# Log decays and norm factors kept sixteen times in DRAM: spread loads that read sixteen places instead of one

## The chip, the core and the metric

The kernel runs on one core of a Trainium2 chip. The core has a matmul engine (PE, with weight loads shown apart as PEld), a vector engine (DVE), an activation engine (ACT), a general engine (POOL) and a sequencer that only issues transfers (SP). Transfers between DRAM and the on-chip memory run on sixteen DMA engines; most are issued by SP, some by POOL, a few by ACT. The on-chip memory has 128 partitions, and a matmul leaves its result in one of eight accumulation banks (here four named acc and four named dn). The metric is device time in microseconds, lower is better; a measurement is the median of several executions, and one execution more is taken with the profiler.

## The reference, cut to what matters

One decoder layer over 1024 positions of 2048 channels, in float32. The parts that the change touches are the first norm and the gated delta rule:

```python
h = rmsnorm(x, ln_g[l])                 # x * rsqrt(mean(x*x) + eps) * g, g has 2048 entries
proj = h @ w_in[l]                      # split into the groups' columns
...
g = -jnp.exp(dn_a_log[l]) * jax.nn.softplus(d_a + dn_dt_bias[l])    # log decays, 8 heads
...
g_cum = jnp.cumsum(g, axis=-1)
diff = g_cum[..., :, None] - g_cum[..., None, :]
decay = jnp.exp(jnp.where(tri, diff, -jnp.inf))
a = jnp.where(strict, jnp.einsum('bhnid,bhnjd->bhnij', kb, k) * decay, 0.0)
...
attn_intra = jnp.where(tri, jnp.einsum('bhnid,bhnjd->bhnij', q, k) * decay, 0.0)
q_g = q * jnp.exp(g_cum)[..., None]
```

Beside the delta rule there is a gated token mix (group A), attention into 256 memory tokens (group C), an output projection with a residual and a final norm. In all of these the matrix products carry nearly all of the work.

## The kernel before

Every float32 product is made of three products of rounded halves: an operand is split into a high part (a cast on ACT: whi, ahi, zh) and a low part (a subtraction on DVE: wlo, alo, zl), and PE adds hi*hi, hi*lo and lo*hi in a bank. Sequence positions go in two halves of 512; the large projections are made as seven products of sums of blocks instead of eight products.

The stages, in order of time: the keys and values of the memory (16 steps of k over w_mem_kv, 512 KB of weights each, in the rotating buffers wraw and ut); beside them the first norm of the x tiles (squares on ACT, a product of x with the row's factor and with gb, the spread ln_g, on DVE, a transpose on PE into the banks dn, a copy on ACT into tn, a split into ahi and alo); then the projections of the first four heads of the delta rule, the decays, and the per-head work; then the large projections with the scan of the delta rule between their products; at the end the output projection and the final norm.

The program text records operations; a planner (`Plan.issue`) sorts them by ready time, rank, and an estimated cost for each, and writes every engine's queue in that order. Engines execute their queues in order, so the planner's sequence decides who waits behind whom. `rank` sets a class (small goes first), `behind` holds an operation until another one in the planner's reckoning, without a wait on the chip. The estimates of a transfer depend on its size, on its longest run of bytes and on its issuer. All operations share one line in the profile, L297, the line of the planner that issues them, so rows are told apart by the names of their tiles.

The change touches two places:

- ln_g. Four loads on SP (`gb[c]`, the tiles zg) bring 512 entries each to all 128 partitions with `partition_broadcast(P)`: each of 128 partitions reads the same 2 KB of DRAM. They are recorded after step k = 3 of the memory's keys, with rank 2, and `prep` uses them for every x tile.
- the log decays. `decays(hf, a)` works out the cumulative log decays of a half for all heads, transposes them to rows (`gr`, 32 partitions of 128) and stores them on SP in `gcs[hf]` (gcd in the profile, 8 heads by 512 positions). For each head and half `qk` then issues on POOL a load of one row of 512 to all 128 partitions (`er`, the tile E): sixteen loads in all. ACT makes vs, the exponential of E, POOL masks E, and ACT makes the decay between positions from it.

Around the first place the queue of SP holds, in this order: x tile 0 (vs), weights of k = 7 (ut), weights of k = 8 (wraw, which waits until DVE has used up the buffer's former content), the four loads of ln_g (zg), weights of k = 9 (wraw), the four loads of x tile 1 (kd), weights of k = 10 and 11 (ut).

Of the kernel before, what the change touches and what calls it, by code (L numbers as in the profile page):

```python
# [17 lines left out]
P = 128  # L18
D = 2048
# [3 lines left out]
HT = 512  # L23
# [3 lines left out]
NG, NH, NX = 4, 8, 4  # L27
# [33 lines left out]
class Plan:  # L61
# [27 lines left out]
    @contextmanager  # L89
    def rank(self, cls):  # L90
        old, self.cls = self.cls, cls
        yield
        self.cls = old

    @contextmanager
    def behind(self, op):
        old, self.gate = self.gate, op
        yield
        self.gate = old
# [201 lines left out]
def kernel(  # L301
# [29 lines left out]
    V, S, G, PE, Q = R.dve, R.act, R.pool, R.pe, R.sp  # L331
# [5 lines left out]
    def DT(shape, name, dt=F32):  # L337
        return dr.tile(list(shape), dt, name=name, tag=name)[:]
# [38 lines left out]
    def rep(ap, n):  # L377
        return ap.unsqueeze(1).to_broadcast([ap.shape[0], n, ap.shape[1]])
# [42 lines left out]
    def tpb():  # L421
        turn["tp"] += 1
        return acc[2 + turn["tp"] % 2]

    h0_d = DT([KT, P, HT], "h0d")
    hT_d = DT([KT, P, HT], "hTd")

# [62 lines left out]
    gb = [ring["zg"]() for _ in range(4)]  # L490
# [4 lines left out]
    def load_mem(q):  # L495
        for mt in range(2):
            Q.dma_start(mem_rows[mt][q], mem[mt * P : (mt + 1) * P, q * HT : (q + 1) * HT])

    def kv_parts(k):
        n = XW if k == 0 else 2 * XW  # L500
        return [slice(i, i + n) for i in range(0, 2 * XW, n)]

    def load_kv(k):
        for sl in kv_parts(k):
            Q.dma_start(kvraw[k % 4][:, sl], w_mem_kv[k * P : (k + 1) * P, sl])
# [7 lines left out]
    y1 = C([P, 2 * NT, 32], "y1")  # L513
    rows = y1.rearrange("p c m -> p (c m)")[:, 0:P]
    mrow = rows[0:16]
    with rank(2):
        load_mem(0)
        S.dma_start(mrow, mem_norm_g[0].rearrange("(c p) -> c p", p=P))
        for k in range(4):
            load_kv(k)  # L520
            if k == 1:
                load_mem(1)
    with rank(3):
        load_mem(2)
        load_mem(3)
# [69 lines left out]
    for k in range(KT):  # L595
        mh, ml = mhl[k // 4]
        if k >= 4:
            with rank(3):
                load_kv(k)
        hi, lo = kvhi[k % 2], kvlo[k % 2]  # L600
        with rank(2):
            for sl in kv_parts(k):
                raw = kvraw[k % 4][:, sl]
                S.activation(hi[:, sl], raw, AF.Copy, scale=gcol[:, k : k + 1])
                V.scalar_tensor_tensor(lo[:, sl], raw, gcol[:, k : k + 1], hi[:, sl], op0=ALU.mult, op1=ALU.subtract)
        kk = k % 4
        for h in range(NX):
            sl = slice(h * P, (h + 1) * P)
            triple(ka[h][:, :NMEM], (hi[:, sl], lo[:, sl]), (mh[:, kk], ml[:, kk]), k == 0, k == KT - 1)
        for mt in range(2):  # L610
            sl = slice(mt * P, (mt + 1) * P)
            triple(va[mt], (mh[:, kk, sl], ml[:, kk, sl]), (hi[:, XW:], lo[:, XW:]), k == 0, k == KT - 1)
        kvmark.append(R.ops[-1])
        if k == 3:
            with rank(2), behind(kvmark[-1]):
                for c in range(4):
                    Q.dma_start(gb[c], ln_g[0, c * HT : (c + 1) * HT].partition_broadcast(P))
        if k in (1, 4, 8):
            with behind(kvmark[-1]):
                mhl.append(spread_mem(len(mhl)))  # L620
        if k == 1:
            load_x(0, "vs", kvmark[1:2] * 4)
        if k == 3:
            for mt in range(2):
                rm.append(C([P, 1], f"rm{mt}"))
                V.tensor_copy(rm[mt], row_scale(mem_rows[mt]))
        if k == 4:
            load_x(1, "kd", kvmark[4:5] * 4)
        if k == 5:
            prep(0, put0(0), spare)  # L630
        if k == 7:

            dg, rmb = (ring["E"]()[:, 0:NMEM] for _ in range(2))
            for mt in range(2):
                V.tensor_scalar(dg[:, mt * P : (mt + 1) * P], ident, rm[mt], None, op0=ALU.mult)
            pt = spare()
            PE.matmul(pt[:, 0:NMEM], ones, dg, start=True, stop=True)
            S.copy(rmb, pt[:, 0:NMEM])
        if k == 9:
            prep(1, put0(1), spare)  # L640
            load_x(2, "kT", (kvmark[6], kvmark[7], kvmark[7], kvmark[8]))
        if k == 13:
            load_x(3, "qT", (kvmark[10], kvmark[11], kvmark[11], kvmark[12]))
            with rank(2):
                prep(2, put0(2), spare)
# [6 lines left out]
    for mt in range(2):  # L652
        t = [ring["ai"](F32R) for _ in range(2)]
# [9 lines left out]
    for h in range(NX):  # L663
        t = ring["vs"](F32R).rearrange("p (s m) -> p s m", s=2)
# [105 lines left out]
    gr = C([NT * NH, P], "gr")  # L770
# [3 lines left out]
    r3, ww = ([steps[:, i * P : (i + 1) * P] for i in two] for two in ((0, 1), (2, 3)))  # L774
    scs = [C([P, 7, NT, NH], f"sc{hf}") for hf in range(2)]
    sct = C([P, 5, NT, NH], "sct")
    gcs = [DT([NH, HT], f"gcd{hf}") for hf in range(2)]
    scan_banks, work = dnr.bufs[0:2], over(dnr.bufs[2:4])

    def decay_mm(a, k):  # L780
# [4 lines left out]
    def decays(hf, a):  # L785

        NU = NT * NH
        ab = ring["tn"]()[0:32]
        with rank(1):
            S.copy(ab, a[0:32])  # L790
        sc = scs[hf]
        beta, gg, gc, egl, edk, ngb, w0 = (sc[:, i] for i in range(7))
        w1, w2, w3, w4, egc = (sct[:, i] for i in range(5))
        tp = tpb()
        for tt in range(NT):
            PE.transpose(tp[:, tt * 32 : tt * 32 + 32], ab[:, tt * P : (tt + 1) * P], ident[0:32, 0:32])
        tpv = tp[:, 0 : NT * 32].rearrange("p (t c) -> p t c", c=32)
        with rank(1):
            S.copy(abt, tpv[:, :, 0 : 2 * NH])
            V.tensor_tensor(out=abt, in0=abt, in1=tpv[:, :, 2 * NH :], op=ALU.add)  # L800
            S.activation(beta, abt[:, :, NH:], AF.Tanh, scale=0.5)
            V.tensor_scalar(beta, beta, 1.0, 0.5, op0=ALU.add, op1=ALU.mult)
            V.tensor_tensor(out=w0, in0=abt[:, :, 0:NH], in1=rep(dtb, NT), op=ALU.add)
            S.activation(w1, w0, AF.Abs)
            S.activation(w1, w1, AF.Exp, scale=-1.0)
            V.tensor_scalar(w2, w1, 2.0, None, op0=ALU.add)
            V.reciprocal(w2, w2)
            V.tensor_tensor(out=w2, in0=w1, in1=w2, op=ALU.mult)
            V.tensor_tensor(out=w3, in0=w2, in1=w2, op=ALU.mult)
            V.tensor_scalar(w4, w3, 1.0 / 15.0, None, op0=ALU.mult)  # L810
            for c in (13.0, 11.0, 9.0, 7.0, 5.0, 3.0):
                V.scalar_tensor_tensor(w4, w4, 1.0 / c, w3, op0=ALU.add, op1=ALU.mult)
            V.scalar_tensor_tensor(w4, w4, 1.0, w2, op0=ALU.add, op1=ALU.mult)
            V.tensor_scalar(w0, w0, 0.0, None, op0=ALU.max)
            V.scalar_tensor_tensor(w0, w4, 2.0, w0, op0=ALU.mult, op1=ALU.add)
            V.tensor_tensor(out=gg, in0=w0, in1=rep(nal, NT), op=ALU.mult)
            dp = tpb()
            ggf = gg.rearrange("p t h -> p (t h)")
            PE.matmul(dp[:, 0:NU], utri, ggf, start=True, stop=True)
            PE.matmul(dp[:, NU : 2 * NU], ones, ggf, start=True, stop=True)  # L820
            gcf = gc.rearrange("p t h -> p (t h)")
            V.tensor_copy(gcf, dp[:, 0:NU])
            S.activation(egl.rearrange("p t h -> p (t h)"), dp[:, NU : 2 * NU], AF.Exp)
            V.tensor_tensor(out=edk.rearrange("p t h -> p (t h)"), in0=dp[:, NU : 2 * NU], in1=gcf,
                            op=ALU.subtract)
            S.activation(edk, edk, AF.Exp)
            S.activation(egc, gc, AF.Exp)
            V.tensor_scalar(ngb, egc, -1.0, None, op0=ALU.mult)
            V.tensor_scalar(w0, gc, -1.0, None, op0=ALU.mult)
            tp = tpb()  # L830
            byh = sct[:, 0].rearrange("p t h -> p (t h)")
            V.tensor_copy(byh.rearrange("p (h t) -> p t h", t=NT), dp[:, 0:NU].rearrange("p (t h) -> p t h", h=NH))
            PE.transpose(tp[0:NU, 0:P], byh, ident)
            V.tensor_copy(gr, tp[0:NU, 0:P])
            Q.dma_start(gcs[hf].rearrange("h (t p) -> (h t) p", p=P), gr)


    todo = []
# [83 lines left out]
    def qk(h, hf, q, k, hs, gt):  # L922
# [10 lines left out]
        er = ring["E"]()  # L933
        e = tok(er)
        with behind(begun.get((h, hf))):
            G.dma_start(er, gcs[hf][h].partition_broadcast(P))
        vs = tok(ring["vs"]())
        S.activation(vs, e, AF.Exp)
        G.affine_select(out=e, in_=e, compare_op=ALU.is_ge, fill=NEG, base=0,
# [686 lines left out]
    for n, (tag, to) in enumerate((("gt", mkT), ("inv", mv))):  # L1626
        for i in range(NX // 2):
            t = ring[tag](F32R).rearrange("p (h s m) -> p h s m", h=2, s=2)
# [190 lines left out]
```

## Time and profile before

| what | value |
|---|---|
| median of 3 runs | 1629.0 us (1626.97 to 1629.74) |
| profiled execution | 1630.94 us, its span 1629.2 us |
| PE busy | 1611.6 us, 99% of the span |
| DVE, ACT, POOL busy | 1262.2, 1027.0, 300.3 us |
| DMA moved | 428.94 MB, mean 263 GB/s |
| loads of ln_g (zg) | 4 of 256 KB, median 6.3 us from issue to landing |
| loads of the decays (E) | 16 of 256 KB, median 6.7 us |

A row of the timeline has the start in us from the span's start, the time that it took in us, the engine (SPq: SP's queue), the operation, the tiles as out<-in with their shapes, how many of them follow each other, and in brackets how long the engine stood idle before it and what ended that. A row of the table of windows has the stretch, its length, then for PE, PEld, DVE, ACT and POOL the busy time and the number of instructions, then the TensorE clock granted (1.00 is full), the share of the DMA engines that was busy, and GB/s. A row of the list of transfers has the tiles, the issuer, the count, the KB of each and the median us from issue to landing. A group of instructions has, behind its count, the busy time in us and the mean of one in ns, then the idle time before them with its causes. Matmuls are pipelined, so the 0.39 us of one and the 0.226 us from start to start are both right.

### The profile page before, as it was taken

The page shows a single profiled execution, that of the slowest core. Times are in us where ns is not written, and L with a number is a line of the kernel's source. Part 1 is how long each engine was busy: PE and PEld are TensorE (multiplying, and loading weights), DVE is VectorE, ACT ScalarE, POOL GpSimd, SP SyncE. Part 2 cuts the span into 40 slices and gives each one's busy share as a digit, 9 for nine tenths or more (in the row PEclk, how much of TensorE's full clock was granted, in tenths as well). Part 3 has the DMA queues.
Part 4 walks back from the last instruction along what each step waited for, and adds up shares of the span by engine and source line. Part 5 has one row for each costly group of instructions (what it writes and reads, how often), then busy time and mean ns, then how long its engine had stood idle before and what let it go on. Part 6 is the DMA issues. An engine that isn't in the chain of part 4 may idle for free.

```text
span 1629.2 us, 26133 instructions
## 1 busy us (share of the span) xinstructions
PE 1611.6 (99%) x8576; PEld 1354.8 (83%) x8576; DVE 1262.2 (77%) x2100; ACT 1027.0 (63%) x2217; POOL 300.3 (18%) x482
## 2 busy tenths in 40 slices
PE   8999999999999999999999999999999999999997
PEld 8988888888888888888888788888888888888886
DVE  5966787879756567899988897768768888789775
ACT  6767675765475457888685346766666775344355
POOL 0101220351452010225235005330100000000001
PEclk9999999999999999999999999999999999999999
DMA  9867898988977785689878977878968869688646
GB/s 309 241 179 225 280 301 251 278 282 309 359 257 242 261 283 190 204 286 368 281 243 253 320 228 241 266 265 296 319 201 274 282 218 364 207 273 293 218 146 239
DMA packets 277227, 428.94 MB, mean 263 GB/s; under 512 B 31017, under 2 KB 102242, under 8 KB 277090
## 3 DMA queue, kind: packets, MB, share of 16 engines
q1 hardware_dynamic: 254338, 366.81, 68.7%
q0 software_dynamic: 22144, 59.40, 10.9%
q8 instruction: 67, 1.10, 0.3%
q10 hardware_dynamic: 608, 1.06, 0.2%
q14 instruction: 70, 0.57, 0.1%
HBM read 339.57 MB, written 87.06 MB: 262 GB/s over the span
## 4 chain that ended last, share of the span: by engine, by line
PE 89%; DMA 6%; DVE 2%; issue 1%; ACT 1%; SPq 1%; POOLq 0%; POOL 0%; DVEq 0%; ACTq 0%
PE acc L297 69%; PE dn L297 20%; DMA wraw<-in_w_in_dram 1%; SPq L297 1%; DMA vs<-od 1%; DMA kT<-in_mem_dram 1%; DVE alo L297 0%; DMA wraw<-hTd 0%; DVE y L297 0%; DMA ai<-in_w_in_dram 0%; DMA kd<-in_x_dram 0%; DMA y<-in_w_in_dram 0%; DMA wraw<-in_w_out_dram 0%; DMA pd<-y 0%; DMA wraw<-in_w_mem_kv_dram 0%
## 5 line engine op out<-in xcount | busy, mean ns | idle before, releaser
L297 PE MATMUL acc<-ahi,whi 128*128 128x512 f32 (+1 forms) x1512 | 535.5, 392 | 0.0
L297 PE MATMUL acc<-ahi,wlo 128*128 128x512 f32 (+1 forms) x1144 | 446.9, 391 | 0.0
L297 PEld LDWEIGHTS acc<-ahi,whi 128*128 128x128 f32 x1512 | 283.2, 188 | 53.9
L297 PE MATMUL acc<-alo,whi 128*128 128x512 f32 (+1 forms) x776 | 302.1, 389 | 0.2 <-DVE alo L297 0.2
L297 PEld LDWEIGHTS acc<-ahi,wlo 128*128 128x128 f32 x1144 | 215.2, 188 | 41.0 <-DVE wlo L297 0.4
L297 ACT CAST whi<-wraw 128x512 fp32r<-128x512 f32 (+1 forms) x167 | 134.2, 804 | 129.1 <-PE acc L297 86.7
L297 DVE TENSOR_TENSOR wlo<-wraw,whi 128x512 fp32r<-128x512 f32 (+1 forms) x167 | 154.0, 922 | 60.7 <-ACT whi L297 56.9
L297 ACT CAST ahi<-raws 128x1024 fp32r<-128x1024 f32 x130 | 136.3, 1049 | 61.2 <-PE acc L297 26.9
L297 PEld LDWEIGHTS acc<-alo,whi 128*128 128x128 f32 x776 | 146.0, 188 | 27.6 <-DVE alo L297 0.6
L297 PE MATMUL acc<-ahi,zl 128*128 128x512 f32 x376 | 148.2, 394 | 0.0
L297 PE MATMUL acc<-alo,zh 128*128 128x512 f32 x376 | 148.2, 394 | 0.0
L297 PE MATMUL acc<-ahi,zh 128*128 128x512 f32 x376 | 148.1, 394 | 0.0
L297 POOL TENSOR_TENSOR small<-small,mhalf 128x1 f32<-128x1 f32 x26 | 18.0, 696 | 590.9 <-DVE small L297 578.0
L297 DVE TENSOR_TENSOR alo<-raws,ahi 128x1024 fp32r<-128x1024 f32 x65 | 79.3, 1220 | 19.7 <-ACT ahi L297 19.5
L297 DVE TENSOR_TENSOR ahi<-raws,ahi 128x1024 fp32r<-128x1024 f32 x65 | 79.2, 1219 | 18.2 <-ACT ahi L297 17.9
L297 DVE TENSOR_TENSOR alo<-y,ahi 128x1024 fp32r<-128x1024 f32 x65 | 79.2, 1219 | 15.7 <-ACT ahi L297 15.4
L297 ACT CAST ahi<-y 128x1024 fp32r<-128x1024 f32 x65 | 68.1, 1048 | 35.1 <-PE dn L297 19.2
L297 PEld LDWEIGHTS acc<-ahi,zl 128*128 128x128 f32 x376 | 70.7, 188 | 13.8
L297 PEld LDWEIGHTS acc<-ahi,zh 128*128 128x128 f32 x376 | 70.7, 188 | 13.8
L297 PEld LDWEIGHTS acc<-alo,zh 128*128 128x128 f32 x376 | 70.7, 188 | 13.8
L297 PE MATMUL acc<-whi,ahi 128*128 128x512 f32 x232 | 79.7, 391 | 0.0
L297 PE MATMUL dn<-whi,ahi 128*128 128x512 f32 x216 | 74.1, 389 | 0.0
(422 smaller groups left out, 3414.3 us busy)
## 6 DMA issues: line engine op xcount, KB each, us to landing
wraw<-in_w_in_dram SPq DMA_DIRECT2D x268, 256.0 KB, 4.0
raws<-sd SPq DMA_DIRECT2D x150, 256.0 KB, 4.1
y<-in_w_in_dram SPq DMA_DIRECT2D x92, 256.0 KB, 4.7
y<-sd SPq DMA_DIRECT2D x75, 256.0 KB, 3.6
wraw<-in_w_out_dram SPq DMA_DIRECT2D x64, 256.0 KB, 4.7
raws<-h0d SPq DMA_DIRECT2D x54, 256.0 KB, 5.1
y<-in_w_out_dram SPq DMA_DIRECT2D x33, 256.0 KB, 4.8
sd<-zg SPq DMA_DIRECT2D x32, 256.0 KB, 4.0
```

What stands on the lines that cost most here:

```text
L297: o.fn(*o.args, **o.kw)
```

## The change

ln_g is first copied sixteen times into a DRAM buffer of 16 rows by 2048 (`lng_d`), by one transfer on SP at the start, recorded after the second block of weights. The four spread loads read from it: partition p reads row p mod 16. The buffer of the decays gets a leading dimension of 16; the two stores write each row to sixteen places, reading `gr` sixteen times, and each E load reads its head's row from the sixteen places in turn.

```diff
+    COPIES = 16
...
+    lng_d = DT([COPIES, D], "lngd")
     with rank(2):
         load_mem(0)
         S.dma_start(mrow, mem_norm_g[0].rearrange("(c p) -> c p", p=P))
         for k in range(4):
             load_kv(k)
             if k == 1:
                 load_mem(1)
+                Q.dma_start(lng_d, ln_g[0].partition_broadcast(COPIES))
...
             with rank(2), behind(kvmark[-1]):
                 for c in range(4):
-                    Q.dma_start(gb[c], ln_g[0, c * HT : (c + 1) * HT].partition_broadcast(P))
+                    Q.dma_start(gb[c], lng_d[:, c * HT : (c + 1) * HT].partition_broadcast(P // COPIES))
...
-    gcs = [DT([NH, HT], f"gcd{hf}") for hf in range(2)]
+    gcs = [DT([COPIES, NH, HT], f"gcd{hf}") for hf in range(2)]
...
-            Q.dma_start(gcs[hf].rearrange("h (t p) -> (h t) p", p=P), gr)
+            Q.dma_start(gcs[hf].rearrange("r h (t p) -> (h t) r p", p=P), rep(gr, COPIES))
...
-            G.dma_start(er, gcs[hf][h].partition_broadcast(P))
+            G.dma_start(er, gcs[hf][:, h].partition_broadcast(P // COPIES))
```

As the planner sorts anew whenever an operation, a price or a dependence changes, the order of other operations moves too. In SP's new queue the copy to lngd stands seventh, and the four loads of ln_g stand ahead of the weights of k = 8; the first load of x tile 1 stands between the weights of k = 8 and k = 9.

## The prediction

> **What bounds the kernel now.** I read the page first (busy time, slices, chain), then the table of windows, then single rows of PE, ACT, SP and DVE at the places where PE waits and at those that the change touches.
>
> ```profile
> span 1629.2 us, 26133 instructions
> ...
> PE 1611.6 (99%) x8576; PEld 1354.8 (83%) x8576; DVE 1262.2 (77%) x2100; ACT 1027.0 (63%) x2217; POOL 300.3 (18%) x482
> ...
> PE 89%; DMA 6%; DVE 2%; issue 1%; ACT 1%; SPq 1%; POOLq 0%; POOL 0%; DVEq 0%; ACTq 0%
> ```
>
> PE is busy for 99% of the span and makes 89% of the chain. It is the bound from end to end, so the change can be worth only what it opens or closes in PE's few gaps. The undisturbed rate is 443 matmuls in 100 us, 226 ns each:
>
> ```profile
> 1400.00:1500.00 100.00, 100.00 (x443) 82.81 (x442) 80.24 (x105) 44.81 (x66) 0.00 (x0) 1.00 0.79 261
> ```
>
> The largest gap stands beside the spread loads of ln_g. The rows are PE's, ACT's, DVE's and SP's in order of time, then two windows whose last columns are granted clock, DMA share and GB/s:
>
> ```profile
> 34.40 0.40 PE L297 MATMUL dn<-whi,inv 128*128 128x512 f32 x1
> 36.73 0.66 PE L297 MATMUL dn<-ident,vs 128*128 128x128 f32 x4 [1.93 <-ACT tn L297]
> ...
> 33.83 0.63 ACT L297 ACTIVATE jk<-kd 128x512 bf16<-128x512 f32 x1 [4.34 <-DMA kd<-in_x_dram]
> 34.46 1.13 ACT L297 ACTIVATE whi<-wraw,gcol 128x1024 fp32r<-128x1024 f32 x1
> 35.50 0.61 ACT L297 ACTIVATE jk<-kd 128x512 bf16<-128x512 f32 x1
> 36.11 0.56 ACT L297 COPY tn<-dn 128x512 f32<-128x512 f32 x1
> ...
> 20.89 1.28 DVE L297 SCALAR_TENSOR_TENSOR wlo<-wraw,gcol,whi 128x1024 fp32r<-128x1024 f32 x1 [0.50 <-ACT whi L297]
> ...
> 15.31 1.85 SPq L297 DMA_DIRECT2D vs<-in_x_dram  x4
> 18.84 0.33 SPq L297 DMA_DIRECT2D ut<-in_w_mem_kv_dram  x1
> 22.21 0.33 SPq L297 DMA_DIRECT2D wraw<-in_w_mem_kv_dram  x1
> 22.59 2.49 SPq L297 DMA_DIRECT2D zg<-in_ln_g_dram  x4
> 25.18 0.38 SPq L297 DMA_DIRECT2D wraw<-in_w_mem_kv_dram  x1
> 25.59 3.63 SPq L297 DMA_DIRECT2D kd<-in_x_dram  x4
> ...
> 22.00:32.00 10.00, 10.00 (x69) 9.06 (x68) 7.40 (x14) 7.10 (x15) 1.10 (x2) 1.00 0.88 262
> 37.00:42.00 5.00, 5.00 (x26) 4.69 (x25) 3.35 (x6) 4.87 (x10) 0.00 (x0) 0.66 0.94 241
> ```
>
> Read backwards: PE stands idle for 1.93 us until ACT copies a bank (tn) at 36.11. ACT comes to that copy late because its order puts squares of the second x tile (kd) ahead of it, and the first of them waited 4.34 us for its load. That load went out behind four spread loads of ln_g (zg), 1 MB in all, and these behind the wraw refill, which SP held until DVE's wlo ended at 22.17. Right after the gap the granted clock is 0.66 for 5 us: 0.34 x 5 = 1.7 us lost. Gap and slow clock together are 3.6 us.
>
> **The change, part by part**
>
> *The copy lngd.* One new transfer from DRAM to DRAM, 128 KB written and as much read, seventh in SP's queue, ahead of two weight loads, three mem loads and all that follows. No row shows a transfer from DRAM to DRAM. From below: zero, if it fits between others. From above: 256 KB at the rate of a full stretch, 256/398 = 0.64 us, for all that is behind it.
>
> ```profile
> 12.00:18.00 6.00, 6.00 (x43) 5.49 (x43) 2.07 (x4) 4.15 (x8) 0.55 (x1) 1.00 1.05 398
> ...
> 16.35 1.14 ACT L297 ACTIVATE whi<-ut,gcol 128x1024 fp32r<-128x1024 f32 x1
> 17.39 1.05 ACT L297 CAST gt<-dn 128x512 fp32r<-128x512 f32 x2
> ...
> 18.32 0.28 PE L297 MATMUL acc<-gt,whi 128*128 128x256 f32 x1
> 18.86 0.38 PE L297 MATMUL acc<-gt,wlo 128*128 128x256 f32 x1 [0.15 <-DVE wlo L297]
> ```
>
> In the new order ACT's whi<-ut of the fourth weight block comes after the two gt copies instead of before. It would end near 18.5 (the 2.2 us of the three, in another order) plus the 0.3 to 0.6 us by which the DMAs ahead are late, and PE wants it at 18.32. So PE loses 0.5 to 0.8 us here; I take 0.7, nearer the full queue, since the DMA share is 1.05.
>
> *The spread loads of ln_g.* Same 1 MB, same four issues. What moves is their place: in the new program SP issues them before the wraw refill, so they no longer sit behind DVE's end at 22.17 and can follow the issue of 18.84. Each SP transfer also waits for the one eight places before it (the program says so); the latest of those is an x load issued at 15.31 to 17.2, and such loads land 6.9 us after their issue (row below, kd). So I estimate issues from 19.2 to some 22, up to 3 us earlier. They now need lngd's landing too, but that was issued some 14 us before. The refill keeps its time (DVE frees it), the first kd load moves from 25.59 to about 22.6, the next three follow the second refill as before. With the same 6.9 us to landing, the first kd tile is there at 29.5 instead of 33.83, and the second, issued near 25.6, at 32.5. Its square (0.6) and the copy (0.56) then end near 33.7, before PE, done with its product at 34.63 (34.40 + 0.226), wants the bank. I take the 1.93 us as closed. With the pause the slow clock after it goes: 1.7 us. What is late next is the second copy, which needs one more kd tile (33.0) and ends near 34.9; PE, 0.7 us later from the start-up, reaches it at about 35.3.
>
> Is a load from sixteen places itself faster? Rows for both: the 1 MB lies in a stretch of 262 GB/s (above), yet the spread of final_g, also from one place, lies in one of 381 and lands sooner than ordinary loads.
>
> ```profile
> 1352.00:1358.00 6.00, 6.00 (x28) 4.93 (x27) 3.88 (x5) 3.79 (x7) 0.00 (x0) 1.00 1.05 381
> ...
> zg<-in_ln_g_dram SPq DMA_DIRECT2D x4, 256.0 KB, 6.3
> ...
> fg<-in_final_g_dram SPq DMA_DIRECT2D x4, 256.0 KB, 5.7
> ...
> kd<-in_x_dram SPq DMA_DIRECT2D x6, 256.0 KB, 6.9
> ...
> h0d<-tn SPq DMA_DIRECT2D x8, 256.0 KB, 5.7
> ...
> E<-gcd POOLq DMA_DIRECT2D x16, 256.0 KB, 6.7
> ```
>
> So I count no gain from the places as such: between 0 and what 10 us at 262 instead of 381 GB/s would give, 3.1 us, I take the lower end, since final_g's rows are the same form. All of it that could come would serve the same gap, which the earlier issue closes already.
>
> *The decays.* The two stores gcd<-gr grow from 16 to 256 KB in pieces of 512 B; h0d<-tn (5.7 us to landing) is the like. Before, POOL issued the E load 3.4 us after SP's store (rows below); with 5.7 us to landing instead it goes at most 2.3 us later. POOL waits for that in order; behind it on POOL stand only operations that need E. The sixteen E loads have the same bytes and sixteen places instead of one; their price is bounded like that of zg. What covers them:
>
> ```profile
> 99.37 1.43 SPq L297 DMA_DIRECT2D gcd<-gr  x1
> ...
> 102.77 1.28 POOL L297 DMA_DIRECT2D E<-gcd  x2 [4.44 <-ACT tn L297]
> ...
> 115.42 0.63 ACT L297 ACTIVATE vs<-E 128x512 f32<-128x512 f32 x1
> ...
> 789.61 0.54 POOL L297 DMA_DIRECT2D E<-gcd  x1
> ...
> 796.81 0.63 ACT L297 ACTIVATE vs<-E 128x512 f32<-128x512 f32 x1
> ```
>
> From issue to use there are 12.7 us in the first case and 7.2 in the tightest, against 6.7 to land: a load 2.3 us later is still covered at 115. At 789 the store is long done and only the load counts. Nothing is gained or lost on PE. Without the cover, each us of lateness would be a us of ACT.
>
> *The order of everything else.* The planner sorts all operations anew. By the built program, the order is the same from about two thirds of PE's instructions on; before that small groups move. Largest: the early inverse ends some 5 splits (DVE's subtractions into wlo, zl, alo and ahi, one for every dozen products) later, and PE's first scan chain comes 66 products (66 x 0.226 = 15 us) later. That can close or open gaps such as these; I put it at zero and keep both ends.
>
> ```profile
> 456.64 1.05 PE L297 MATMUL dn<-states,kT 128*128 128x128 f32 x4 [0.88 <-ACT vs L297]
> ...
> 925.71 1.13 PE L297 MATMUL dn<-wsT,el 128*128 128x128 f32 x8 [1.68 <-DMA el<-vd]
> ```
>
> **Sum.** +0.7 - 1.9 - 1.7 = -2.9 us. The profiled execution took 1630.94 us (1629.2 in its span, 1.7 around it), 1.9 above the median of the three runs, 1629.0. So its like would take 1628.0, and the median 1626.1. A measurement of this kernel can tell about 0.2%, 3.3 us, from no change; the forecast lies just inside that.
>
> A page of the Trainium skill bears on the clock: "TensorE: Matmul & The Clock Gate", Part 1, says that the clock is halved after an idle window of about 3.4 us. The trace differs: 0.66 followed a pause of 1.93 us. By the page alone the slow clock wouldn't hang on this pause and would stay, and the sum would be -1.2 (1627.8); I go by the row.
>
> **The rivals**
>
> *DVE becomes the bound (slower).* Between DVE's 288th and 348th split (838 to 1008 us of the trace), the new order holds 91 operations of 512 columns instead of 83 and 8 more small ones, work that slid there from earlier. Priced by these rows, 8 x 0.70 + 8 x 0.16 = 6.9 us:
>
> ```profile
> 838.00:911.00 73.00, 73.00 (x349) 60.42 (x348) 62.39 (x111) 46.10 (x90) 26.85 (x43) 1.00 0.82 263
> 911.00:975.00 64.00, 62.32 (x286) 51.62 (x285) 58.44 (x105) 27.86 (x33) 4.41 (x8) 1.00 0.80 266
> ...
> L297 DVE TENSOR_TENSOR wlo<-wraw,whi 128x512 fp32r<-128x512 f32 x96 | 67.3, 702 | 38.3 <-ACT whi L297 34.8 <-DMA zg<-hTd 2.6 <-PE acc L297 0.5
> ```
>
> For it: DVE is busy 58.4 of 64 us there. Against: 10.6 and 5.6 us of idle time are left in these two windows. It decides once the added work exceeds the idle time that lies in the right places; if all of it reaches PE, -2.9 + 6.9 = +4.0, 1633.0.
>
> *The spread loads take longer and the gap stays (no change).* Their source now has the repetition, eight, as its outermost step. If a transfer were cut by that step, four loads would have half of the sixteen queues: 1 MB at half of 398 GB/s is 5.3 us instead of 2.6. Against: every spread load of before has 128 outermost, so no row shows it; and the earlier start gives back 3 us. The gap then shrinks to about 1.2 and the slow clock stays: +0.7 - 0.7 = 0, 1629.0. The Trainium skill states such a rule, "DMA: Bandwidth & Descriptors", section "Rules for kernel authors": a leading zero-step repetition of c copies confines a transfer to at most c queues; no run here shows it yet.
>
> *Other gaps close as well (clearly faster).* If the later scan chain also spares waits like the 0.88 and 1.68 us above, -2.9 - 2.6 = -5.5, 1623.5.
>
> *Other gaps open.* The same with the sign turned, at several unnamed places: about +4, 1633.
>
> **Chances.** Forecast 0.40 (0.22 of it beyond the bound, 0.18 within), other gaps close 0.13, the gap stays 0.14 (0.07 within, 0.07 slower), DVE 0.20, other gaps open 0.13. That makes faster 0.35, same 0.25, slower 0.40. The range reaches from 1621.5 (all of the faster case and 2 us) to 1635.5 (DVE's case and 2.5 us); the forecast's own range is 1623 to 1628.5.
>
> **What would show it.** Right: in the profile after, zg issues ahead of 22 us, no wait of ACT above 1 us for kd, no PE idle above 0.5 us near 35, clock 1.00 in 37 to 42; a PE wait of under 1 us near 18.5; E landing before its use everywhere. Wrong: PE waits on DVE after 838, zg landing above 8 us, a slow clock elsewhere.

## The result and the profile after

The changed kernel takes 1641.75 us in the median (1640.09 to 1644.81), the kernel before on the same chip 1627.99 (1626.83 to 1629.74). The ratio is 1.0088, its 95% interval 1.0072 to 1.0103: slower by some 14 us, outside the predicted range. The profiled execution took 1640.09 us.

The page of the changed kernel, with the span, the first row of busy times and the chain:

```profile
span 1638.3 us, 26122 instructions
...
PE 1615.6 (99%) x8576; PEld 1356.5 (83%) x8576; DVE 1261.6 (77%) x2100; ACT 1025.5 (63%) x2215; POOL 289.6 (18%) x482
...
PE 85%; DMA 7%; issue 3%; DVE 2%; ACT 2%; POOL 1%; SPq 0%; POOLq 0%; DVEq 0%; ACTq 0%
```

PE is still the bound, but its share of the chain has gone from 89 to 85%, and what came in is waiting: DMA, issue, ACT. PE's busy time is 4 us longer at the same number of instructions: it ran at half clock for longer. The timeline of the changed kernel shows the two places that cost most, the prologue and the time near 930 us:

```profile
18.25 0.38 PE L297 MATMUL acc<-gt,whi 128*128 128x256 f32 x1
33.44 0.40 PE L297 MATMUL dn<-whi,gt 128*128 128x512 f32 x1
37.12 0.66 PE L297 MATMUL dn<-ident,vs 128*128 128x128 f32 x4 [3.29 <-ACT tn L297]
...
33.99 0.63 ACT L297 ACTIVATE jk<-kd 128x512 bf16<-128x512 f32 x1 [5.01 <-DMA kd<-in_x_dram]
...
19.96 2.64 SPq L297 DMA_DIRECT2D zg<-lngd  x4
23.30 0.61 SPq L297 DMA_DIRECT2D kd<-in_x_dram  x1
...
932.92 2.05 PE L297 MATMUL dn<-wsT,el 128*128 128x128 f32 x8 [3.10 <-DMA el<-vd]
...
927.53 0.33 SPq L297 DMA_DIRECT2D el<-vd  x1
```

The spread loads of ln_g are issued 2.6 us earlier than before, at 19.96, as predicted, and the first kd load 2.3 us earlier, at 23.30. But ACT gets that tile no sooner: 33.99 against 33.83. PE's pause, 1.93 us before, is 3.29. Near 930 us PE waits 3.10 us (1.68 before) for the tile el, values of the delta rule that come back from the DRAM buffer vd. The chain ahead of that wait, in order of time (start, us, what passed in it), is:

```profile
916.42 5.34 DMA y<-in_w_in_dram
...
922.15 5.37 DMA kd<-in_w_in_dram
...
927.53 5.25 DMA el<-vd
```

So the load of el goes out only when a kd load has landed, eight transfers ahead of it on SP, and that load went out behind one that had waited in the same way for a y load. In the chain of the kernel before el goes out at 920.12 behind SP's issuing alone, with no landing ahead of it. The windows of the changed kernel (columns as in the section on the profile before):

```profile
37.00:42.00 5.00, 4.88 (x25) 4.58 (x26) 3.07 (x6) 4.78 (x11) 0.00 (x0) 0.66 0.90 295
932.00:939.00 7.00, 6.08 (x21) 5.34 (x22) 2.55 (x4) 0.00 (x0) 0.00 (x0) 0.51 0.92 329
838.00:911.00 73.00, 71.43 (x338) 58.53 (x337) 62.66 (x116) 46.08 (x98) 31.79 (x55) 1.00 0.87 284
911.00:975.00 64.00, 60.37 (x268) 49.82 (x267) 53.88 (x99) 26.36 (x31) 3.36 (x6) 0.95 0.77 245
1400.00:1500.00 100.00, 100.00 (x443) 82.81 (x442) 79.19 (x103) 43.60 (x64) 0.00 (x0) 1.00 0.77 258
```

The slow clock of 37 to 42 us is still there, and a second one, twice as long (6.83 us at half clock), follows the wait at 932. In the undisturbed window 1400 to 1500 there are 443 matmuls, as before: nothing has become slower where PE isn't starved. The issues of the changed kernel give the landing times:

```profile
E<-gcd POOLq DMA_DIRECT2D x16, 256.0 KB, 7.4
...
kd<-in_x_dram SPq DMA_DIRECT2D x4, 256.0 KB, 10.6
```

E takes 7.4 us (6.7 before); the x loads behind the spread of ln_g (second row, issues of 20 to 36 us alone) take 10.6, where the prediction counted 6.9. With the same order and loads of one place (x1 below) they take 6.4.

### The profile page after: what moved, and what is told of

It is laid out like the page before. It is cut to its first block, busy times and chain, and to the rows that moved or that the text cites. A ratio compares the mean times of both kernels' runs of the same rounds, so it can differ in the third digit from the quotient of the medians.

```text
span 1638.3 us, 26122 instructions
## 1 busy us (share of the span) xinstructions
PE 1615.6 (99%) x8576; PEld 1356.5 (83%) x8576; DVE 1261.6 (77%) x2100; ACT 1025.5 (63%) x2215; POOL 289.6 (18%) x482
## 4 chain that ended last, share of the span: by engine, by line
PE 85%; DMA 7%; issue 3%; DVE 2%; ACT 2%; POOL 1%; SPq 0%; POOLq 0%; DVEq 0%; ACTq 0%
PE acc L297 64%; PE dn L297 20%; DMA y<-in_w_in_dram 1%; DMA kd<-in_x_dram 1%; DMA y<-h0d 1%; DVE wlo L297 0%; DMA ut<-in_x_dram 0%; DVE y L297 0%; DMA tdrearly<-inv 0%; DMA kT<-in_mem_dram 0%; DMA ut<-udrearly 0%; DMA wraw<-in_w_mem_kv_dram 0%; ACT y L297 0%; DMA ut<-in_w_mem_kv_dram 0%; DMA kd<-in_w_in_dram 0%
```

## The experiments

Two theories. *Order*: the copy of ln_g and the dearer stores make the planner sort the program anew, and the new order is worse at its waits. *Transfers*: a load whose source repeats eight times in its outermost step lands later. All ratios are to the kernel before, measured on the same chip; one thousandth is 1.6 us.

| run | order | spread loads read | median us | ratio (95%) |
|---|---|---|---|---|
| changed kernel | new | 16 places, 8 rounds | 1641.75 | 1.0088 (1.0072 to 1.0103) |
| x1_one_place | new | 1 place | 1639.17 | 1.0071 (1.0057 to 1.0085) |
| x2_sixteen_outer | new | 16 places, step of 16 outermost | 1639.76 | 1.0071 (1.0051 to 1.0092) |
| x3_before_order | old | 16 places, 8 rounds | 1639.05 | 1.0071 (1.0058 to 1.0083) |
| x4_before_order_outer | old | 16 places, step of 16 outermost | 1631.67 | 1.0027 (1.0016 to 1.0038) |
| x5_order_lng_only | old | ln_g 8 rounds, decays 1 place | 1633.25 | 1.0038 (1.0026 to 1.0050) |
| x6_order_decays_only | old | decays 8 rounds, ln_g 1 place | 1633.38 | 1.0033 (1.0021 to 1.0045) |
| x7_one_place_el_later | new, el products later | 1 place | 1632.45 | 1.0028 (1.0014 to 1.0041) |
| x8_before_zg_early | old, zg and one kd load earlier | 1 place | 1625.73 | 0.9989 (0.9980 to 0.9998) |
| x9_changed_el_later | new, el products later | 16 places, 8 rounds | 1637.81 | 1.0062 (1.0050 to 1.0074) |
| x10_thirty_two_places | old | 32 places, 4 rounds | 1647.23 | 1.0116 (1.0102 to 1.0131) |
| x11_two_places | old | 2 places, 64 rounds | 1627.41 | 0.9999 (0.9990 to 1.0008) |
| x12_decays_alone | own new order | decays 8 rounds, ln_g as before | 1638.20 | 1.0071 (1.0056 to 1.0086) |

The expectations speak of mean landings over the sixteen E loads; the rows below have medians.

**New order, other reads.** x1 reads one of the sixteen places; stores, copy and order stay:

```diff
-Q.dma_start(gb[c], lng_d[:, c * HT : (c + 1) * HT].partition_broadcast(P // COPIES))
+Q.dma_start(gb[c], lng_d[0, c * HT : (c + 1) * HT].partition_broadcast(P))
-G.dma_start(er, gcs[hf][:, h].partition_broadcast(P // COPIES))
+G.dma_start(er, gcs[hf][0, h].partition_broadcast(P))
```

> Every instruction stands in the changed kernel's order, the stores still write sixteen places and ln_g is still copied first, but each spread load reads one place (the first of the sixteen). Theory 'order' (the time was lost because the planner sorted the whole program anew, above all in the wait for the el tile's vd values near 930 us and the halved clock behind it): nothing comes back, 1638 to 1645 us, and the product that ran at 945 us in the changed kernel is still some 8 us behind the kernel before. Theory 'transfers' (reading sixteen places in eight-fold steps lands later): back to 1628 to 1631 us, E lands some 1 us earlier after its issue, and the pause near 37 us shrinks from 3.3 to about 2 us.

x2 keeps the sixteen places and puts them outermost:

```diff
-Q.dma_start(gb[c], lng_d[:, c * HT : (c + 1) * HT].partition_broadcast(P // COPIES))
+Q.dma_start(gb[c], rep(lng_d[:, c * HT : (c + 1) * HT], P // COPIES))
-G.dma_start(er, gcs[hf][:, h].partition_broadcast(P // COPIES))
+G.dma_start(er, rep(gcs[hf][:, h], P // COPIES))
```

> The changed kernel's order and its sixteen places, but a load walks the places in its outer step (sixteen) and repeats each eight times inside it, instead of eight rounds over sixteen places. Theory 'order': 1638 to 1645 us, as the changed kernel. Theory 'an outer step of eight uses only half of the chip's DMA engines': the four zg loads and the kd loads behind them land 2 to 3 us earlier, the pause near 37 us goes from 3.3 to under 2 us, the E loads land 1 us earlier, and the time falls by 3 to 10 us.

The timeline of x1, its window at the prologue, and its E row:

```profile
33.70 0.60 PE L297 MATMUL dn<-ident,vs 128*128 128x128 f32 x4
...
30.52 0.63 ACT L297 ACTIVATE jk<-kd 128x512 bf16<-128x512 f32 x1 [1.51 <-DMA kd<-in_x_dram]
32.39 0.63 ACT L297 ACTIVATE jk<-kd 128x512 bf16<-128x512 f32 x1
...
934.81 2.05 PE L297 MATMUL dn<-wsT,el 128*128 128x128 f32 x8 [3.92 <-DMA el<-vd]
...
37.00:42.00 5.00, 5.00 (x32) 4.29 (x31) 4.36 (x8) 5.00 (x10) 0.56 (x1) 1.00 1.02 307
...
E<-gcd POOLq DMA_DIRECT2D x16, 256.0 KB, 6.2
```

With one place the pause is gone altogether, PE goes from 33.47 to the transposition at 33.70 without idle time, and the clock is full from 37 to 42. Yet the time hardly moves. The wait at el is still there (3.92 us, 6.83 us at half clock behind it). This execution, the slowest of its six (1642.73 us), also has two pauses that the changed kernel's profile lacks, 1.89 us at 450.50 and 1.55 us at 498.30, each with 3.41 us at half clock behind it. x2 has no pause in the prologue either (clock 1.00 in 37 to 42), and 3.04 us of wait at el. So the new order alone costs about 0.7%, as the theory of order expected; the step of eight is what keeps the pause, as the theory of transfers expected, but in this order the time differs by less than the intervals can tell (1.0088 against 1.0071).

**Old order, new transfers.** The planner is made to price the gcd store as one copy and not to see the copy of ln_g; every engine then gets the old order, with the copy put in on SP:

```diff
+                if key.startswith("lngd"):
+                    continue
...
+            if out.tensor.name.startswith("gcd"):
+                o.moves /= 16
+            if out.tensor.name.startswith("lngd"):
+                o.cost = o.moves = 0.0
```

> All transfers as changed, but the planner prices the gcd store as one copy and doesn't see the copy of ln_g, so that every engine gets the order of the kernel before, with the copy of ln_g put in. Theory 'order': the 945 us loss is gone; 1627 to 1632 us, what is left being the start-up, where the zg loads are slower by up to 3 us. Theory 'transfers': 1638 to 1644 us, although the order is the old one.

x4 is x3 with the reads of x2.

> The kernel before in its order, with sixteen places read in an outer step of sixteen. Theory 'order': 1626 to 1630 us, no change from the kernel before within 0.2%, since neither landing times of E nor of zg set the end. Theory 'sixteen places are read faster if all DMA engines take part': E and zg land 1 us or more earlier than in the kernel before and the time falls to 1622 to 1626 us.

The timeline of x3, its window at the second place, and its E loads, all sixteen and then the two issued between 438 and 450 us (8.2 us in the kernel before):

```profile
39.26 1.12 PE L297 MATMUL dn<-ident,vs 128*128 128x128 f32 x4 [5.03 <-ACT tn L297]
...
456.81 1.22 PE L297 MATMUL dn<-states,kT 128*128 128x128 f32 x4 [5.51 <-DVE states L297]
...
455.87 0.69 DVE L297 TENSOR_TENSOR qT<-qT,y 128x512 f32<-128x512 f32 x1 [5.01 <-DMA y<-in_w_in_dram]
...
443.95 0.33 SPq L297 DMA_DIRECT2D y<-in_w_in_dram  x1
...
455.00:462.00 7.00, 5.19 (x51) 4.39 (x54) 5.21 (x11) 2.79 (x8) 0.00 (x0) 0.54 1.02 346
...
E<-gcd POOLq DMA_DIRECT2D x16, 256.0 KB, 7.9
...
E<-gcd POOLq DMA_DIRECT2D x2, 256.0 KB, 11.2
```

So the theory of order falls as the only cause: in the old order the transfers alone cost as much, 0.71%. The places are others. The pause of the prologue is 5.03 us, since zg is issued late here, and slow. Near 457 us PE waits 5.51 us for the scan's states, which DVE couldn't copy because it stood 5.01 us at a product that wants y, a slice of w_in. That y isn't a spread load: it was issued at 443.95, beside two E loads that took 11.2 us, and landed 11.9 us later, where the same load took 6.4 in the kernel before. In these runs a slow load makes its neighbours late. With the step of sixteen outermost (x4) 0.44 of the 0.71% goes, but not all; in its profile the wait at the states is 2.39 us with a half clock behind it. Its 1631.67 us lie above what either theory gave. Why sixteen rounds still cost 0.27%, x11 with sixty-four nothing, isn't settled; the two E loads of the burst near 441 us take 9.3 us in x4 (8.2 in the kernel before).

**The two halves of the transfers**, in the old order: x5 is x3 with the E loads of x1, x6 is x3 with the zg loads of x1.

> The kernel before's order with the copy of ln_g; only the four zg loads read sixteen places in eight-fold steps, the decay loads E read one place. Theory 'eight-fold loads land later, each at its own place': the pause at the first transposition of x stays at 4 to 5.5 us near 39 us with a half clock of 3.41 us behind it, but the wait for the scan's states near 457 us falls from 5.7 to between 1 and 2.6 us and its half clock goes; 1630 to 1634 us. Rival 'the stores and the copy cost it': about 1639 us, as with both parts.

> The kernel before's order with the copy of ln_g; only the E loads read sixteen places in eight-fold steps, zg reads one place. Theory 'eight-fold loads land later': the mean landing of the sixteen E loads stays near 8.0 us (6.4 in the kernel before), the wait near 457 us stays at 4.5 to 6 us with its half clock, the pause near 36 us is 1.2 to 2.2 us; 1632 to 1637 us. Rival 'the stores and the copy cost it': about 1639 us.

The timeline and the E row of x5, then of x6:

```profile
39.93 1.11 PE L297 MATMUL dn<-ident,vs 128*128 128x128 f32 x4 [5.33 <-ACT tn L297]
...
E<-gcd POOLq DMA_DIRECT2D x16, 256.0 KB, 6.8
```

```profile
35.22 0.66 PE L297 MATMUL dn<-ident,vs 128*128 128x128 f32 x4 [0.59 <-ACT tn L297]
449.54 0.71 PE L297 MATMUL dn<-states,kT 128*128 128x128 f32 x4 [2.00 <-DVE states L297]
...
E<-gcd POOLq DMA_DIRECT2D x16, 256.0 KB, 8.3
```

Each half is slow at its own place: 0.38 and 0.33%, together the 0.71 of x3. Both runs keep the copy and the stores, so if the parts add up nothing is left for these, within the 0.2% that such a sum is good to. x6's profile shows a smaller wait than expected (2.00, not 4.5 to 6, and no half clock there); that execution was the fastest of its five, 1630.21 us at a median of 1633.38, so where the others lose the rest isn't shown.

**The size of the outer step.** x10 and x11 are x3 with `COPIES = 32` and `COPIES = 2` (the planner's division of the price to match): four and sixty-four rounds.

> The kernel before's order, thirty-two places, each spread load in four rounds over thirty-two places. Theory 'a load is spread over as many DMA engines as its outer step counts': the mean landing of E goes on from 6.4 (128 rounds of one place) and 8.0 us (eight rounds) to 10 us or more, the pause near 39 us grows beyond 7 us, 1645 to 1665 us. Rival 'it is the reading of several places that is slow, whatever the step': 8 to 8.5 us, 1638 to 1642 us.

> The kernel before's order, two places, each spread load in sixty-four rounds over two places. Theory 'outer step': sixty-four is plenty, E lands in 6.3 to 7.0 us in the mean, 1626 to 1631 us. Rival 'several places are slow': between one place and sixteen, above 7 us, 1630 us or more.

The timeline and the E row of x10, then of x11:

```profile
45.87 1.12 PE L297 MATMUL dn<-ident,vs 128*128 128x128 f32 x4 [9.89 <-ACT tn L297]
471.52 1.35 PE L297 MATMUL dn<-states,kT 128*128 128x128 f32 x4 [3.95 <-ACT vs L297]
...
E<-gcd POOLq DMA_DIRECT2D x16, 256.0 KB, 9.3
```

```profile
35.02 0.66 PE L297 MATMUL dn<-ident,vs 128*128 128x128 f32 x4 [0.85 <-ACT tn L297]
...
E<-gcd POOLq DMA_DIRECT2D x16, 256.0 KB, 6.7
```

With 4, 8, 16, 64 and 128 rounds E lands in 9.3, 7.9, 6.8, 6.7 and 6.7 us, and the time follows: 1.0116, 1.0071, 1.0027, 0.9999, 1. x3 and x4 read the same sixteen places and differ in the outer step alone, so most of the cost goes with that step; whether x4's last 0.27% does, or goes with the number of places, is open. And no read of several places is clearly faster than one of one place: E takes 6.7 us in x11 and in the kernel before.

**The wait at el.** In x7 the four products of the first el load get a later ready time in the planner; the order ahead of 925 us stays. x9 is the same edit on the changed kernel.

```diff
+        R.slow += 5000.0 if (hf, g) == (0, 0) else 0.0
         for tt in range(NT):
             PE.matmul(hand[:, tt * P : (tt + 1) * P], vg[:, tt], wsT[g], start=True, stop=True)
+        R.slow -= 5000.0 if (hf, g) == (0, 0) else 0.0
```

> The changed kernel's order with loads of one place, but the planner puts the four wsT products that wait for the first el load some 20 products (4.5 us) later; everything ahead of about 925 us is as it was. Theory 'the new order costs its time at this one wait': 4.1 us of wait and 3.4 to 6.8 us of half clock (half of it lost) go, 1631 to 1634 us. Rival 'the new order loses in many places, or the next wait takes over': 1636 to 1641 us.

> The changed kernel as it is, eight-fold loads too, but the four wsT products of the first el load stand some 20 products later. Theory 'the wait at the el load and its half clock are the one large cost of the new order': 3.1 us of wait and 3.4 us lost at half clock go, 1633 to 1637 us, some 3 us above the same edit on one-place loads (1632.45). Rival 'in the changed kernel another wait behind it takes over': 1639 us or more.

The timeline of x7, then the timeline and windows of x9:

```profile
909.72 0.66 PE L297 MATMUL dn<-ident,ut 128*128 128x128 f32 x4 [1.29 <-ACT vs L297]
928.65 1.06 PE L297 MATMUL dn<-wsT,el 128*128 128x128 f32 x8
932.71 1.16 PE L297 MATMUL dn<-wsT,tn 128*128 128x128 f32 x8 [1.16 <-DVE el L297]
```

```profile
37.60 0.66 PE L297 MATMUL dn<-ident,vs 128*128 128x128 f32 x4 [3.83 <-ACT tn L297]
499.21 0.62 PE L297 MATMUL dn<-ident,vs 128*128 128x128 f32 x2 [1.54 <-ACT vs L297]
938.87 1.06 PE L297 MATMUL dn<-wsT,el 128*128 128x128 f32 x8
...
37.00:42.00 5.00, 4.40 (x29) 4.04 (x30) 3.41 (x6) 5.00 (x12) 0.00 (x0) 1.00 0.86 279
496.00:503.00 7.00, 5.46 (x24) 4.43 (x23) 3.38 (x6) 4.66 (x13) 1.77 (x3) 0.78 0.83 301
```

The wait goes in both. In x7 that is worth 0.43% (7.0 us) of the order's 0.71, within what was expected; in x9 0.26% (4.2 us), and its 1637.81 us lie above the expected 1637 and below its rival's 1639. Each of these differences is good to some 0.2%. The 0.28% that x7 keeps isn't settled: its profile has waits of 1.29 and 1.16 us that the kernel before doesn't have, but they don't sum to 4.6 us. Its eight executions lie in two groups, four from 1627.0 to 1630.9 us and four from 1634.0 to 1635.0, and the profile is of the first; what the second group loses isn't shown. The pauses of x1 near 450 and 498 us, of the same order, are candidates.

**One half of the change alone**, planned freely: x12 takes the change's lines on the decays and leaves ln_g as it was.

> Only the decays are kept sixteen times, planned as the planner does it (its own new order from 105 us on); ln_g is read as in the kernel before. Theory: the E loads land in 7 to 8 us in the mean, the pause near 36.7 us is as before (it lies ahead of the first E), and the new order is as near its waits as the changed kernel's; 1634 to 1641 us. Rival 'the copy of ln_g brought all of the new order's cost': 1630 to 1634 us, as with the decays alone in the old order (1633.4).

The timeline and the E row of x12:

```profile
35.14 0.66 PE L297 MATMUL dn<-ident,vs 128*128 128x128 f32 x4 [0.85 <-ACT tn L297]
928.98 2.05 PE L297 MATMUL dn<-wsT,el 128*128 128x128 f32 x8 [3.65 <-DMA el<-vd]
...
E<-gcd POOLq DMA_DIRECT2D x16, 256.0 KB, 8.0
```

The decays' part alone gives another new order, and it has the same wait at el: 3.65 us. So this half is enough to bring it about; ln_g's half alone wasn't planned freely. The row at 35.14 tells something of the prediction, too: up to there x12 does just what the kernel before does, and its pause is 0.85 us, not 1.93, with the clock at 1.00 from 37 to 42.

**A faster version.** x8 is the kernel before, with five loads moved by hand on SP:

```diff
+        kds = [o for o in self.ops if o.eng == "sp" and o.args[0].tensor.name.startswith("kd")]
+        min(kds, key=lambda o: o.at).at -= 1000.0
+        for o in self.ops:
+            if o.eng == "sp" and o.args[0].tensor.name.startswith("zg") and o.args[1].tensor.name.startswith("in_ln_g"):
+                o.at -= 3000.0
         self.ops.sort(key=lambda o: (o.at, o.idx))
```

> The kernel before with one place in every load, no copy, its order on every engine, but the four zg loads stand ahead of one weight load and the first kd load ahead of another on SP, as in the changed kernel. The prediction's second and third step (the pause near 36.7 us closes and the half clock behind it goes): 1623 to 1625 us. Rival 'the loads displaced are then late': no gain, 1626 to 1629 us, with the pause moved to a weight block.

The window of x8 at the prologue:

```profile
37.00:42.00 5.00, 5.00 (x34) 4.43 (x33) 4.45 (x7) 4.97 (x11) 0.16 (x1) 1.00 1.04 314
```

PE has no idle time and full clock there. The gain is 0.11% (0.02 to 0.20), 1.8 us, just clear of no change. It is about half of what the prediction's steps would give, and 1625.73 us lies between what was expected and the rival's range.

## Why the prediction was wrong

- *The start-up, +0.7.* Not there in the profiled execution of the changed kernel: the product at 18.25 us has no idle time ahead of it. But x9, the same up to there, has the predicted wait, 0.74 us for ACT's whi (row below), and x1 has 0.68, x7 0.47, x2 none. So the term was about right, in some executions.

```profile
18.16 0.39 PE L297 MATMUL acc<-gt,whi 128*128 128x256 f32 x1 [0.74 <-ACT whi L297]
```

- *The earlier spread loads, -1.93.* The issue times came out (19.96 to 22.60 us predicted as 19.2 to some 22; first kd load 23.30 for 22.6). The step that failed is the next one, "with the same 6.9 us to landing": 10.6 us behind eight-fold loads. With one place read (x1) the step holds where it counts: the square of the second kd tile starts at 32.39 (tile predicted at 32.5), and there is no pause. The first tile came at 30.5, not 29.5, since it took 8.0 us; in the prediction's own rows, 25.59 to 33.83, it had taken 8.2, not 6.9. PE did not wait for that one.
- *The slow clock, -1.7.* It stayed with the pause. Where the pause does go, x8 measures both terms together at 1.8 us, not 3.6. The prediction took one execution's pause and half clock for a fixed cost; x12, the same up to there, shows 0.85 us and no half clock.
- *Places as such, 0.* Right: 6.7 us for one place and for two, and no run that reads several places is faster than the kernel before.
- *E covered, 0.* Failed. The prediction compared E's landing with E's use, at 115 and 789 us. It didn't look at 443 us, where two E loads are issued in a burst, nor at the loads beside them: the y of w_in is what came late in x3. In the old order this half costs 0.33%.
- *The new order, "I put it at zero and keep both ends".* The largest miss: 0.71% (x1, with the copy and the stores in it), of which some 0.43 is one wait (x7). The very row that was quoted for it, 1.68 us at el, became 3.10, with 6.83 us at half clock behind it. The ends kept for it, -2.6 us (other gaps close) to +6.9 us (DVE), were too narrow.
- *The rivals.* "The spread loads take longer and the gap stays" had the mechanism: the outer step of eight. The rule of the Trainium skill, "DMA: Bandwidth & Descriptors", section "Rules for kernel authors", agrees with the landing times of x10, x3 and x11 (9.3, 7.9 and 6.7 us); no profile here shows which engines a transfer used. The rival was priced on zg alone, from an average rate, and set at no change; the E loads and the loads beside them were left out. "DVE becomes the bound" explains little: PE is idle 1.6 of the 73 us from 838 on (1.47 of it one wait for DVE's ai, at 851.95, which the kernel before doesn't have), and of the 3.6 us idle in the next window 3.1 are the wait at el. "Other gaps open" came true at a named place.

The parts don't add up: the order alone costs 0.71%, the transfers alone 0.71, both together 0.88 (each good to some 0.15%). The earlier zg of the new order hides part of the slow loads (in the old order their pause is 5.0 to 5.3 us, in the new 3.3 to 3.8); the rest of the overlap wasn't taken apart.

## What to carry to other kernels

Look at the outermost step of a transfer's access pattern before counting its bytes: here loads of eight and of four rounds landed late, and so did what was issued beside them. Where a planner orders a tightly packed kernel, a small new operation far from a wait can re-time that wait; undo the order and the edit apart before judging either. And don't book a half clock seen in one execution as a fixed cost.

## What the runs showed of the hardware

The half clock comes on a fixed grid. In each of these executions the stretches at half clock begin whole multiples of 3.413 us apart (in the changed kernel at 37.71 and 932.00 us: 262 periods), and where the grid lies differs between executions. Cut along that grid, the fourteen profiles give, from 20 us to the last product, fifteen periods at full clock behind which it was halved. Eleven of them held 1.93 us or more of PE idle time (of 3.41), and no period with that much was spared; four held 1.54 to 1.74 us, and five others with 1.53 to 1.92 us were spared. So a pause is dear or cheap by where it falls: x9's pause of 3.83 us at 37 us lies half in one period and half in the next, 1.92 us in each, and the clock stays at 1.00 (its window above); its pause of 1.54 us at 499 us is followed by 3.41 us at half clock (0.78 in its window). The Trainium skill, "TensorE: Matmul & The Clock Gate", Part 1, has this window as 3413 ns long and free-running, which agrees; the idle time that is enough, about half of a period, is what these runs add.
